# MLA attention on one core: products of P with V of two query tiles in one place of TensorE's order, and transposed P copied back into its own tile

## The chip, the cores and the metric

The kernel runs on one core of a Trainium2 chip. The metric is device time in microseconds for one execution, the median over several runs. The profile is of one execution of the same program.

## The reference, cut to what matters

One residual block of an encoder, 512 tokens, width 1024: attention in two head groups side by side (8 MLA heads of 96/64, 4 differential heads), output projection, a gated convolutional feed-forward part, and a gate from per-layer embeddings. The change touches the MLA heads alone:

```python
q = rms_norm(q, q_g); k = rms_norm(k, k_g)          # 8 heads, 96 wide
q, k = rope on the last 32 columns of each
scale = MLA_QK ** -0.5
allowed = (k_idx[None, :] // CHUNK) <= (q_idx[:, None] // CHUNK)   # CHUNK = 64
logits = einsum('bhqd,bhkd->bhqk', qb, k_t) * scale
logits = where(allowed, logits, NEG_INF)
probs = softmax(logits, axis=-1)
o = einsum('bhqk,bhkd->bhqd', probs, v_t)            # v is 64 wide
```

All in float32, with `SEQ = 512`, `D_MODEL = 1024`, `MLA_HEADS = 8`, `MLA_QK = 96`, `MLA_V = 64`.

## The kernel before, in words

**Tiles and steps.** The 512 queries are four tiles of 128 (t = 0 to 3). By the mask, tile t needs the first (t + 1) * 128 keys. Heads go in pairs (hp = 0 to 3), the two heads of a pair are c = 0, 1. The loop at L840 goes over hp and t; step i = 4hp + t does, in the program's order:

1. `mla_norm` (DVE, L614): P of tile t is multiplied by the reciprocal of its row sums.
2. `mla_logits` of the next tile (TensorE through `mm3`, L157 to L159: three products a block, because each operand is a high and a low part; bank `ml`), and DVE's row maxima (L587 or L590, then L588 or L591).
3. `mla_exp` (ACT, L605): exponentials into the P tile `pm`, with row sums. At t = 2, heads of the next pair are transposed and split between them (`mla_q`, `mla_k`, L559 and L566, banks of the tag `tp`; splits by ACT L185, L188 and DVE L186, L189), at t = 3 two more. In the last pair the first transposes and logits of the differential heads stand there (`d0T`, `d1T` L715, `dl`).
4. `extra` work of that step (splits of later weights L305, squares and scalings of the differential heads' z, L407 and L414), then `pump(n)`: products of the projection z of the differential heads (`zd`, six products of 512 columns each pump) that fill TensorE's time; n is 2 in pairs 0 to 2 and 1 in the last.
5. `mla_T`: P of tile t is transposed on TensorE (L547, bank `pTm`), each head's P in its own bank, or both heads in one bank for t < 2 (`one`). It is copied to a tile `pt` (L550 by ACT, L552 by DVE).
6. `mla_pv` of the tile of the step before (L633): 64-wide V is the stationary operand, transposed P the moving one; head c fills partitions 64c to 64c + 63 of the bank `mo`. A block of 128 keys is four instructions in the trace (two heads, two passes each). After t = 3 ACT copies the bank to `ym` (L636).

**Buffers.** `pm` tiles come from four buffers in a ring (`pm_tile`), `pt` tiles from two (`pt_tile`). A tile with t < 2 takes one of each, a tile with t > 1 two of each. After the loop the differential heads use both rings for their own P.

**What sets the order.** TensorE runs in the order of the program for the whole kernel. DVE, ACT and POOL do so from L217 to L888, which holds this whole stage; a planner places what the program issues after that, and it can put such instructions in idle places of ACT's order inside the stage (casts of the output projection's weights, L150, come from there). DMAs of weights are issued by SP; none is issued by the functions that the diff touches.

Of the kernel before, what the change touches and what calls it, by code (L numbers as in the profile page):

```python
# [22 lines left out]
NT = 4  # L23
# [4 lines left out]
H = 8  # L28
# [66 lines left out]
def hybrid_block(ctx: ExitStack, tc: tile.TileContext, a: dict, out: bass.AP):  # L95
    nc = tc.nc
    V, S, G, TE = nc.vector, nc.scalar, nc.gpsimd, nc.tensor
# [13 lines left out]
    def bank(tag, name):  # L111
        return pp_.tile([P, 512], F32, tag=tag, bufs={"acc": 2, "lg": 3, "tp": 2, "ob": 1}[tag], name=name)

    def tt(name, dtype=F32):
        return att.tile([P, T], dtype, tag="tt", bufs=16, name=name)
# [4 lines left out]
    def pm_tile(name):  # L120
        return att.tile([P, T], F32, tag="pm", bufs=PM, name=name)

    def pt_tile(name):
        return att.tile([P, T], F32, tag="pt", bufs=2, name=name)
# [29 lines left out]
    def mm3(ps, blocks, first=True, last=True, again=False):  # L154
        n = len(blocks)
        for i, (xh, xl, wh, wl) in enumerate(blocks):
            TE.matmul(ps, xh, wh, start=first and i == 0, stop=False, skip_group_check=again)  # L157
            TE.matmul(ps, xh, wl, start=False, stop=False, skip_group_check=again)  # L158
            TE.matmul(ps, xl, wh, start=False, stop=last and i == n - 1, skip_group_check=again)  # L159
# [31 lines left out]
    tsl = [slice(t * P, (t + 1) * P) for t in range(NT)]  # L191
# [208 lines left out]
    def z_flush():  # L400
        while zouts:
            zouts.pop(0)()
# [37 lines left out]
    def pump(n=1):  # L440
        for _ in range(n):
            while fill:
                try:
                    next(fill[0])
                    break
                except StopIteration:
                    fill.pop(0)
# [37 lines left out]
    qn, kv = [], []  # L485
# [54 lines left out]
    pump(FILL_QK)  # L540


    def probs_T(pm, n, name, on_act):

        ps = bank("tp", f"pT{name}")
        for j in range(0, n, P):
            TE.transpose(ps[:, j:j + P], pm[:, j:j + P], ident)  # L547
        pt = pt_tile("pt")
        if on_act:
            S.copy(pt[:, :n], ps[:, :n])  # L550
        else:
            V.tensor_copy(pt[:, :n], ps[:, :n])  # L552
        return pt

    def mla_q(h):
        qh_, ql_, kh_, kl_ = QT[h % 2]
        ps = bank("tp", f"qT{h}")
        for t in range(NT):
            TE.transpose(ps[:QK, tsl[t]], qn[t][:, h, :], ident)  # L559
        split(qh_[:QK], ql_[:QK], ps[:QK], qcol[:QK])  # L560

    def mla_k(h):
        qh_, ql_, kh_, kl_ = QT[h % 2]
        ps = bank("tp", f"kT{h}")
        for t in range(NT):
            TE.transpose(ps[:QK, tsl[t]], kv[t][:, h, :QK], ident)  # L566
        split(kh_[:QK], kl_[:QK], ps[:QK])

    mla, ymn = {}, []

    def mla_logits(hp, t):

        n, one = (t + 1) * P, t < 2
        r = rq[:, 0, t, 2 * hp:2 * hp + 2]
        sums = sm.tile([P, 3, 2], F32, tag="sums", bufs=4, name="sums")
        nm = sums[:, 0]
        ps, pm = [], []
        for c in range(2):
            qh_, ql_, kh_, kl_ = QT[c]
            if c and one:  # L580
                ps.append(full[:, n:2 * n])
            else:
                full = bank("lg", f"ml{hp}{t}{c}")
                ps.append(full[:, :n])
            mm3(ps[c], [(qh_[:100, tsl[t]], ql_[:100, tsl[t]], kh_[:100, :n], kl_[:100, :n])])
            if not one:
                V.reduce_max(nm[:, c:c + 1], ps[c], axis=AX.X, negate=True)  # L587
                V.tensor_tensor(nm[:, c:c + 1], nm[:, c:c + 1], r[:, c:c + 1], op=ALU.mult)  # L588
        if one:
            V.reduce_max(nm, full[:, :2 * n].rearrange("p (c k) -> p c k", c=2), axis=AX.X, negate=True)  # L590
            V.tensor_tensor(nm, nm, r, op=ALU.mult)  # L591
        mla["lg", hp, t] = ps, nm, r
        for c in range(2):
            if c and one:
                pm.append(pmf[:, n:2 * n])
            else:
                pmf = pm_tile("pm")
                pm.append(pmf[:, :n])
        mla["pm", hp, t] = pm, pmf, sums, one

    def mla_exp(hp, t, c):

        ps, nm, r = mla["lg", hp, t]
        pm, pmf, sums, one = mla["pm", hp, t]
        S.activation(pm[c], ps[c], AF.Exp, bias=nm[:, c:c + 1], scale=r[:, c:c + 1], accum_out=sums[:, 1, c:c + 1])  # L605

    def mla_norm(hp, t):

        pm, pmf, sums, one = mla["pm", hp, t]
        ssum, rcp = sums[:, 1], sums[:, 2]  # L610
        for c in range(2):
            if c == 0:
                V.reciprocal(rcp, ssum)
            V.tensor_scalar(pm[c], pm[c], rcp[:, c:c + 1], None, op0=ALU.mult)  # L614

    def mla_T(hp, t):

        n = (t + 1) * P
        pm, pmf, sums, one = mla.pop(("pm", hp, t))
        if one:  # L620
            pt = probs_T(pmf, 2 * n, f"m{hp}{t}", t)
            mla["pt", hp, t] = [pt[:, :n], pt[:, n:2 * n]]
        else:
            mla["pt", hp, t] = [probs_T(pm[c], n, f"m{hp}{t}{c}", c) for c in range(2)]

    def mla_pv(hp, t):

        if t == 0:
            mla["po"] = bank("ob", f"mo{hp}")
        po, pt = mla["po"], mla.pop(("pt", hp, t))  # L630
        for j in range(t + 1):
            for c in range(2):
                TE.matmul(po[64 * c:64 * c + 64, tsl[t]], kv[j][:, 2 * hp + c, 96:], pt[c][:, tsl[j]], start=j == 0, stop=j == t)  # L633
        if t == NT - 1 and hp < H // 2 - 1:
            yn = tt(f"ym{hp}")
            S.copy(yn, po)  # L636
            ymn.append(yn)
# [82 lines left out]
    def diff_logits(h, t):  # L720
        n = (t + 1) * P
        if t == 0:
            df["s0", h] = sm.tile([P, NT], F32, tag="s0", name="s0")
        s0 = df["s0", h][:, t:t + 1]
        (qh_, ql_), (kh_, kl_) = df["qk", h, 0], df["qk", h, 1]
        pms, s1 = [], sm.tile([P, 1], F32, tag="s1", bufs=4, name="s1")
        for m in range(2):
            r = slice(64 * m, 64 * m + 64)
            ps = bank("lg", f"dl{h}{t}{m}")
            mm3(ps[:, :n], [(qh_[r, tsl[t]], ql_[r, tsl[t]], kh_[r, :n], kl_[r, :n])])  # L730
            pm = pm_tile("pmd")
            nm = sm.tile([P, 1], F32, tag="nm", bufs=4, name="nmd")
            V.tensor_tensor_reduce(out=pm[:, :n], in0=ps[:, :n], in1=strips[0][:, h, T - n:], scale=1.0, scalar=3e38, op0=ALU.add, op1=ALU.min, accum_out=nm)  # L733
            S.activation(pm[:, :n], pm[:, :n], AF.Exp, bias=nm, scale=-1.0, accum_out=s0 if m == 0 else s1)  # L734
            pms.append(pm)
        df["pm", h, t] = pms, n, s0, s1
# [53 lines left out]
    HP = H // 2  # L790
# [44 lines left out]
    z13 = z1_hi(3)  # L835
    pump()
    mla_logits(0, 0)
    for c in range(2):
        mla_exp(0, 0, c)
    for hp in range(HP):  # L840
        for t in range(NT):
            i = NT * hp + t
            last = hp == HP - 1
            n = FILL_MLA[hp][t]
            if t:
                mla_norm(hp, t)
            if t < NT - 1:
                mla_logits(hp, t + 1)
            if t == 2:
                for c, (d, m) in enumerate(((diff_T, (0, 0)), (diff_T, (0, 1))) if last else ((mla_q, (2 * hp + 2,)), (mla_k, (2 * hp + 2,)))):  # L850
                    d(*m)
                    mla_exp(hp, t + 1, c)
            elif t < 2:
                for c in range(2):
                    mla_exp(hp, t + 1, c)
            else:
                pump()
                n -= 1
                if last:
                    diff_logits(0, 0)  # L860
                else:
                    mla_q(2 * hp + 3)
                    mla_k(2 * hp + 3)
            if t == 0:
                mla_norm(hp, t)
            for e in extra.get(i, ()):
                e()
            pump(n)
            for e in late.get(i, ()):
                e()  # L870
            mla_T(hp, t)
            z_flush()
            if i:
                mla_pv(*divmod(i - 1, NT))
            if t == 3 and not last:
                mla_logits(hp + 1, 0)
                for c in range(2):
                    mla_exp(hp + 1, 0, c)
# [49 lines left out]
    for b in order[:6]:  # L928
        n = len(early)
# [359 lines left out]
    ts = [token_sums(k) for k in range(K2)]  # L1289
# [279 lines left out]
```

## Time and profile before

| what | value |
|---|---|
| median of 3 runs | 644.8 us (644.76 to 645.9) |
| the profiled execution | 644.82 us |
| its span in the trace | 643.0 us |
| TensorE matmul busy | 632.4 us, 98% |
| DVE, ACT, POOL busy | 486.9, 360.2, 69.2 us |
| products with V in the trace (L633) | 160 instructions, first 78.6, last 156.2 us |
| transposes of P of the MLA heads (L547, pTm) | 80 instructions, 73.8 to 153.0 us |
| granted TensorE clock | full in all slices |

A line of the timeline gives the start, the busy time, the engine, the line of the kernel, the operation, tile written and tiles read, the shape, how many instructions are merged, and in brackets the idle time of the engine before it with what ended it. PE is TensorE's products, PEld its weight loads, DVE is VectorE, ACT ScalarE. The ends of products are modelled, so starts are the better measure there.

### The profile page before, as it was taken

The page shows a single profiled execution, that of the slowest core. Times are in us where ns is not written, and L with a number is a line of the kernel's source. Part 1 is how long each engine was busy: PE and PEld are TensorE (multiplying, and loading weights), DVE is VectorE, ACT ScalarE, POOL GpSimd, SP SyncE. Part 2 cuts the span into 40 slices and gives each one's busy share as a digit, 9 for nine tenths or more (in the row PEclk, how much of TensorE's full clock was granted, in tenths as well). Part 3 has the DMA queues.
Part 4 walks back from the last instruction along what each step waited for, and adds up shares of the span by engine and source line. Part 5 has one row for each costly group of instructions (what it writes and reads, how often), then busy time and mean ns, then how long its engine had stood idle before and what let it go on. Part 6 is the DMA issues. An engine that isn't in the chain of part 4 may idle for free.

```text
span 643.0 us, 10203 instructions
## 1 busy us (share of the span) xinstructions
PE 632.4 (98%) x3900; PEld 556.2 (87%) x3900; DVE 486.9 (76%) x870; ACT 360.2 (56%) x629; POOL 69.2 (11%) x94
## 2 busy tenths in 40 slices
PE   8999999999999999999999999999999999999997
PEld 8988888876777887889999999999999999988886
DVE  6889667887898678988876767676767777759844
ACT  7896567666667355557555545545454545637111
POOL 1514103030000130001000000000100000000000
PEclk9999999999999999999999999999999999999999
DMA  8241612330221437546865656464646554532021
GB/s 304 100 165 37 182 62 66 99 130 2 66 85 49 164 132 228 148 95 157 208 197 117 184 124 199 117 180 116 180 115 182 118 177 115 181 130 66 27 88 50
DMA packets 29912, 82.63 MB, mean 129 GB/s; under 512 B 3100, under 2 KB 4124, under 8 KB 29736
## 3 DMA queue, kind: packets, MB, share of 16 engines
q1 hardware_dynamic: 23816, 69.17, 32.3%
q0 software_dynamic: 5616, 12.33, 11.3%
q8 instruction: 31, 0.51, 0.3%
q10 hardware_dynamic: 432, 0.49, 0.2%
q14 instruction: 17, 0.14, 0.1%
HBM read 77.77 MB, written 5.52 MB: 130 GB/s over the span
## 4 chain that ended last, share of the span: by engine, by line
PE 86%; DVE 7%; ACT 3%; issue 2%; DMA 1%; ACTq 0%; DVEq 0%; SPq 0%
PE dn L157 6%; PE dn L158 6%; PE dn L159 6%; PE gx L159 4%; PE gx L158 4%; PE gx L157 4%; PE zd L157 3%; PE zd L159 3%; PE zd L158 3%; PE g L157 3%; PE g L158 3%; PE g L159 3%; PE pg L159 2%; PE pg L158 2%; PE pg L157 2%; PE o L157 2%
## 5 line engine op out<-in xcount | busy, mean ns | idle before, releaser
L954 DVE TENSOR_TENSOR wSl<-rS,wSh 128x1024 fp32r<-128x1024 f32 x21 | 25.7, 1224 | 43.4 <-ACT wSh L950 43.2
L157 PE MATMUL dn<-ah,hi_dn 128*128 128x512 f32 x144 | 56.2, 391 | 0.0
L158 PE MATMUL dn<-al,hi_dn 128*128 128x512 f32 x144 | 56.2, 391 | 0.0
L159 PE MATMUL dn<-ah,lo_dn 128*128 128x512 f32 x144 | 56.0, 389 | 0.0
L1071 POOL DMA_DIRECT2D rS<-in_w_gu x19 | 22.7, 1194 | 250.2 <-DVE cv L1239 129.9
L950 ACT CAST wSh<-rS 128x1024 fp32r<-128x1024 f32 x21 | 22.0, 1047 | 35.7 <-PE gy L158 35.4
L157 PE MATMUL zd<-hi_d,xh 128*128 128x512 f32 x96 | 39.1, 407 | 0.0
L158 PE MATMUL zd<-lo_d,xh 128*128 128x512 f32 x96 | 37.6, 392 | 0.0
L682 DVE TENSOR_TENSOR x<-x,dn 128x512 f32<-128x512 f32 x44 | 29.9, 679 | 6.1 <-PE dn L159 6.1
L954 DVE TENSOR_TENSOR wTl<-rA,wTh 128x1024 fp32r<-128x1024 f32 x19 | 23.3, 1225 | 13.7 <-ACT wTh L950 13.2
L159 PEld LDWEIGHTS dn<-ah,lo_dn 128*128 128x128 f32 x144 | 27.0, 188 | 5.8
L157 PEld LDWEIGHTS dn<-ah,hi_dn 128*128 128x128 f32 x144 | 27.1, 188 | 5.1
L158 PEld LDWEIGHTS dn<-al,hi_dn 128*128 128x128 f32 x144 | 27.1, 188 | 5.0
L954 DVE TENSOR_TENSOR wAl<-rA,wAh 128x1024 fp32r<-128x1024 f32 x21 | 25.6, 1217 | 2.7 <-ACT wAh L950 2.7
L950 ACT CAST wAh<-rA 128x1024 fp32r<-128x1024 f32 x21 | 22.1, 1050 | 9.7 <-DMA rA<-in_w_gu 9.5
L1242 ACT ACTIVATE cv<-cv 128x512 f32<-128x512 f32 x22 | 13.9, 630 | 23.9 <-DVE cv L1239 23.8
L157 PE MATMUL g<-b2h,wAh 128*128 128x256 f32 (+1 forms) x88 | 26.4, 300 | 0.5 <-ACT g L1195 0.5
L157 PE MATMUL o<-yh,hi_o 128*128 128x512 f32 x64 | 26.8, 419 | 0.0
L734 ACT ACTIVATE pmd<-pmd,nmd 128x128 f32<-128x128 f32 (+3 forms) x32 | 17.9, 560 | 15.1 <-DVE nmd L733 15.0
L159 PE MATMUL g<-b2h,wAl 128*128 128x256 f32 (+1 forms) x88 | 26.2, 297 | 0.0
L158 PE MATMUL g<-b2l,wAh 128*128 128x256 f32 (+1 forms) x88 | 26.2, 297 | 0.0
L1462 ACT ACTIVATE sg<-sg 128x512 f32<-128x512 f32 (+1 forms) x9 | 5.3, 584 | 36.8 <-DVE sg L1461 36.8
(475 smaller groups left out, 2219.1 us busy)
## 6 DMA issues: line engine op xcount, KB each, us to landing
rA<-in_w_gu SPq DMA_DIRECT2D x22, 512.0 KB, 3.7
rS<-in_w_gu SPq DMA_DIRECT2D x22, 512.0 KB, 3.7
rS<-in_w_gu POOLq DMA_DIRECT2D x19, 512.0 KB, 6.1
raw_dn<-in_w_down SPq DMA_DIRECT2D x18, 512.0 KB, 5.9
raw_d<-in_w_d SPq DMA_DIRECT2D x12, 512.0 KB, 3.4
r<-in_w_gu SPq DMA_DIRECT2D x19, 256.0 KB, 5.9
raw_o<-in_w_out SPq DMA_DIRECT2D x8, 512.0 KB, 3.6
rS_pg<-in_w_pg SPq DMA_DIRECT2D x6, 512.0 KB, 4.1
```

Of the source, the lines that this page charges most:

```text
L157: TE.matmul(ps, xh, wh, start=first and i == 0, stop=False, skip_group_check=again)
L158: TE.matmul(ps, xh, wl, start=False, stop=False, skip_group_check=again)
L159: TE.matmul(ps, xl, wh, start=False, stop=last and i == n - 1, skip_group_check=again)
L682: V.tensor_tensor(xb(b), xb(b), ps, op=ALU.add)
L734: S.activation(pm[:, :n], pm[:, :n], AF.Exp, bias=nm, scale=-1.0, accum_out=s0 if m == 0 else s1)
L950: S.copy(h_, src)
L954: V.tensor_tensor(l_, src, _f32(h_), op=ALU.subtract)
L1071: nc.gpsimd.dma_start(sums[f].rearrange("p (i c) -> p i c", i=2), a["w_gu"][f][:, :2048].rearrange("p (i c) -> p i c", i=2)[:, :, :512], a ...
L1242: S.activation(cv, cv, AF.Silu)
L1462: S.activation(sg, sg, AF.Sigmoid)
```

## The change

`mla_pv` takes several tiles, and a table says at which step which tiles' products with V are issued: tiles 0 and 1 at step 4hp + 2, tiles 2 and 3 at step 4hp + 4, in the last pair tile 2 at step 15 and tile 3 behind the loop, as before. So tile 0's and tile 2's products move one step back. Transposed P has to live longer for this. For t < 2, P is now made in a `pt` tile, and its transpose is copied back into it; for t > 1 it is copied back into its two `pm` tiles, except in the last pair, where two `pt` tiles take it as before.

```diff
-    def probs_T(pm, n, name, on_act):
+    def probs_T(pm, n, name, on_act, pt=None):
...
-        pt = pt_tile("pt")
+        pt = pt_tile("pt") if pt is None else pt
...
-                pmf = pm_tile("pm")
+                pmf = pt_tile("pm") if one else pm_tile("pm")
...
-            pt = probs_T(pmf, 2 * n, f"m{hp}{t}", t)
+            pt = probs_T(pmf, 2 * n, f"m{hp}{t}", t, pmf)
...
-            mla["pt", hp, t] = [probs_T(pm[c], n, f"m{hp}{t}{c}", c) for c in range(2)]
+            mla["pt", hp, t] = [probs_T(pm[c], n, f"m{hp}{t}{c}", c, pm[c] if hp < H // 2 - 1 else None) for c in range(2)]
...
-    def mla_pv(hp, t):
+    def mla_pv(hp, *ts):
-        if t == 0:
+        if ts[0] == 0:
             mla["po"] = bank("ob", f"mo{hp}")
-        po, pt = mla["po"], mla.pop(("pt", hp, t))
-        for j in range(t + 1):
-            for c in range(2):
-                TE.matmul(po[64 * c:64 * c + 64, tsl[t]], kv[j][:, 2 * hp + c, 96:], pt[c][:, tsl[j]], start=j == 0, stop=j == t)
-        if t == NT - 1 and hp < H // 2 - 1:
+        po = mla["po"]
+        for t in ts:
+            pt = mla.pop(("pt", hp, t))
+            for j in range(t + 1):
+                for c in range(2):
+                    TE.matmul(po[64 * c:64 * c + 64, tsl[t]], kv[j][:, 2 * hp + c, 96:], pt[c][:, tsl[j]], start=j == 0, stop=j == t)
+        if ts[-1] == NT - 1 and hp < H // 2 - 1:
...
+    pvs = {NT * hp + 2: (hp, 0, 1) for hp in range(HP)} | {NT * hp + 4: (hp, 2, 3) for hp in range(HP - 1)} | {NT * HP - 1: (HP - 1, 2)}
...
-            if i:
-                mla_pv(*divmod(i - 1, NT))
+            if i in pvs:
+                mla_pv(*pvs[i])
```

## The prediction

> **What bounds the kernel now.** I read the page's summary first, then the waits of TensorE, then a table of busy time by stretches, and only then the timeline of the stage that is changed.
>
> ```profile
> span 643.0 us, 10203 instructions
> ...
> PE 632.4 (98%) x3900; PEld 556.2 (87%) x3900; DVE 486.9 (76%) x870; ACT 360.2 (56%) x629; POOL 69.2 (11%) x94
> ...
> PE 86%; DVE 7%; ACT 3%; issue 2%; DMA 1%; ACTq 0%; DVEq 0%; SPq 0%
> ```
>
> TensorE is busy 98% of the span, and 86% of the chain that ended last is TensorE. A time taken out of TensorE's order is therefore a time taken out of the run, unless TensorE then meets a wait. Where it waits today, the view of waits for TensorE says (us in total, times, longest):
>
> ```profile
> PE mo L633 <- DVE pt L552: 0.7, 1, 0.7
> ...
> PE pTm L547 <- DVE st L189: 0.4, 1, 0.4
> PE pTm L547 <- DVE pm L614: 0.3, 1, 0.3
> ```
>
> These three are the only waits at the lines of the change (transposes of P, L547, and products with V, L633). The table of busy time by stretches puts them (columns: stretch, its length, then busy us of each engine):
>
> ```profile
> 118.00:139.00 21.00, 21.00 (x142) 16.98 (x140) 17.12 (x40) 13.97 (x28) 5.80 (x1) 1.00 0.45 148
> 139.00:157.00 18.00, 16.52 (x132) 12.73 (x132) 13.51 (x38) 12.62 (x32) 0.00 (x0) 1.00 0.02 5
> 157.00:220.00 63.00, 61.39 (x372) 48.68 (x371) 53.51 (x150) 39.09 (x97) 4.03 (x4) 1.00 0.24 78
> 220.00:643.00 423.00, 417.20 (x2608) 376.96 (x2606) 311.95 (x432) 210.75 (x316) 27.89 (x23) 1.00 0.50 140
> ```
>
> Up to 139 us, through head pairs 0 to 2, TensorE has no idle time. In 139 to 157, head pair 3, it is idle 1.48 of 18 us: there ACT and DVE set the end. After 157 it is busy again 97 to 99%. So a gain before 139 should count in full, one after it should not, and what is gained by 157 should last to the end.
>
> **What a separate group of products with V costs.** The timeline of TensorE around three places (start, us, what, how many):
>
> ```profile
> 78.06 0.60 PE L547 MATMUL pTm<-ident,pm 128*128 128x128 f32 x4
> 78.59 0.44 PE L633 MATMUL mo<-pt,kvb 128*64 128x128 f32 x4
> 78.96 0.50 PE L157 MATMUL ml<-st 100*128 100x512 f32 x1
> 79.30 0.39 PE L158 MATMUL ml<-st 100*128 100x512 f32 x1
> ...
> 84.10 0.82 PE L547 MATMUL pTm<-ident,pm 128*128 128x128 f32 x6
> 84.84 0.66 PE L633 MATMUL mo<-pt,kvb 128*64 128x128 f32 x8
> 85.43 0.50 PE L157 MATMUL zd<-hi_d,xh 128*128 128x512 f32 x1
> 85.77 0.40 PE L158 MATMUL zd<-lo_d,xh 128*128 128x512 f32 x1
> ...
> 87.37 0.60 PE L566 MATMUL kT<-ident,kvb 128*96 128x128 f32 x4
> 87.72 0.48 PE L157 MATMUL zd<-hi_d,xh 128*128 128x512 f32 x1
> 88.04 0.40 PE L158 MATMUL zd<-lo_d,xh 128*128 128x512 f32 x1
> ```
>
> The third place has four transposes and then a 512-wide product, with no product with V between: 88.04 - 87.37 = 0.67 us from the first transpose to the second wide product. The first place has the same with four product instructions (tile t=0) between: 79.30 - 78.06 = 1.24, so that group costs 0.57. The second has six transposes, 85.77 - 84.10 = 1.67; two transposes more at 0.11 (x4 lasts 0.60, x6 lasts 0.82) make its base 0.89, so its eight instructions (t=1) cost 0.78. From 0.57 to 0.78 are four instructions more: 0.21 to 0.22 for each key block of 128. What is left when the work is taken off is 0.57 - 0.22 = 0.35 and 0.78 - 0.44 = 0.34: a fixed price of about 0.35 us for going from full-width work to 64-wide work and back. The weight loads show where it sits:
>
> ```profile
> 84.84 0.42 PEld L633 LDWEIGHTS mo<-pt,kvb 128*64 128x64 f32 x8 [0.17 <-issue]
> 85.43 0.19 PEld L157 LDWEIGHTS zd<-hi_d,xh 128*128 128x128 f32 x1 [0.17 <-issue]
> ...
> 87.70 0.19 PEld L157 LDWEIGHTS zd<-hi_d,xh 128*128 128x128 f32 x1
> ```
>
> Before the first 64-wide load and before the first full-width load after it nothing is loaded for 0.17 us, with no releaser; from transposes straight to wide products (87.70) there is no such hole. 2 x 0.17 = 0.34 is the fixed price again. Within a group of eight no hole is shown, although it changes column halves and key blocks, so a second query tile appended should cost its 0.22 per block alone.
>
> [...]
>
> **The change part by part.** Steps are i = 4hp + t, 0 to 15.
>
> Products. Before there are 16 groups, one a tile. After there are nine: pairs at i = 2, 4, 6, 8, 10, 12, 14, tile (3,2) alone at 15, tile (3,3) alone behind the loop. Seven groups go (those at i = 1, 3, ..., 13), each to the step behind it; no instruction is added. Gross: 7 x 0.35 = 2.4 us. The moved products (t=0: 0.22, t=2: 0.65 us) pass logits, fill products and transposes on TensorE and nothing on another queue: no DMA belongs to them, SP and POOL issue the same, and the copy of the finished bank to ym stays at its step.
>
> Copies of transposed P. Same engine, same shape, other destination: 0 (a 512-wide one lasts 0.69 on DVE, below, either way). What hides it is that both tiles lie in SBUF; I know no reason for a price of either sign. Their waits change: in head pairs 0 to 2 the copies no longer wait until the products of an earlier tile have freed one of two pt tiles. That gives DVE and ACT time early in a step, which matters below. In head pair 3, tiles 2 and 3 still copy into pt; the copy of (3,2) by DVE now waits for (3,0)'s products, which stand just behind the transposes: 0 to 0.2 us, covered by another split that keeps DVE until then.
>
> New holds. P of tiles 2 and 3 keeps its pm tiles until the pair's products at i = 4hp + 4. The next writer is the exponential of (hp+1, 2), whose logits come later in TensorE's order than those products: 0. For the bank mo the hold is shorter. Behind the waiting exponential on ACT nothing waits longer than it does for the logits.
>
> **Where the 0.35 does not arrive.** At odd i = 3, 7, 11 the products of tile 2 stood between the transposes and the next head pair's logits. Without them logits begin 1.0 us earlier (0.65 work + 0.35), and the next transposes are reached 1.0 earlier, but they need the normalization that DVE makes from those logits. DVE's and TensorE's rows at i = 4, 8 and 12, in that order:
>
> ```profile
> 91.18 0.69 DVE L552 COPY pt<-pTm 128x512 f32<-128x512 f32 x1 [0.96 <-PE mo L633]
> ```
> ```profile
> 113.66 0.69 DVE L552 COPY pt<-pTm 128x512 f32<-128x512 f32 x1 [0.42 <-PE mo L633]
> ...
> 116.42 0.48 DVE L614 TENSOR_SCALAR pm<-pm,sums 128x128 f32<-128x128 f32 x2
> ```
> ```profile
> 117.80 0.38 PE L547 MATMUL pTm<-ident,pm 128*128 128x128 f32 x2
> ```
> ```profile
> 136.14 0.69 DVE L552 COPY pt<-pTm 128x512 f32<-128x512 f32 x1 [0.35 <-PE mo L633]
> 136.96 0.42 DVE L590 TENSOR_REDUCE sums<-ml 128x2 f32<-128x256 f32 x1
> ...
> 140.82 0.43 DVE L552 COPY pt<-pTm 128x256 f32<-128x256 f32 x1 [0.23 <-PE mo L633]
> ...
> 141.89 0.55 DVE L587 TENSOR_REDUCE sums<-ml 128x1 f32<-128x384 f32 x1
> ...
> 147.67 0.74 DVE L189 SCALAR_TENSOR_TENSOR st<-d0T,dcol,st 128x512 fp32r<-128x512 f32 x1
> ```
> ```profile
> 139.33 0.43 PE L547 MATMUL pTm<-ident,pm 128*128 128x128 f32 x2 [0.26 <-DVE pm L614]
> ...
> 140.72 0.44 PE L157 MATMUL ml<-st 100*128 100x384 f32 x1
> ...
> 141.17 0.34 PE L159 MATMUL ml<-st 100*128 100x384 f32 x1
> ...
> 148.47 1.19 PE L547 MATMUL pTm<-ident,pm 128*128 128x128 f32 x6 [0.38 <-DVE st L189]
> ...
> 155.45 1.09 PE L633 MATMUL mo<-pt,kvb 128*64 128x128 f32 x16 [0.74 <-DVE pt L552]
> ```
>
> i = 8: the copy can start its idle 0.42 earlier, and DVE's chain with it, so normalization ends at 116.90 - 0.42 = 116.5. TensorE arrives at 117.80 - 1.0 = 116.8. Still covered by 0.3, and the full 0.35 counts. At i = 4 DVE idles 0.96 before the copy, and its chain can follow almost the whole 1.0.
>
> i = 12: today TensorE already waits 0.26. DVE gains only its idle 0.35 and the 0.13 between the copy's end (136.83) and the reduction (136.96), so the transposes start about 0.45 earlier instead of 1.0; then 0.65 of tile 2's products follow, and the next logits (140.72) come 0.2 later than now. DVE's reduction of them (141.89) starts 0.38 after the first logits are done (141.51), held by DVE's own queue, so it still comes about 0.1 earlier. At i = 13 TensorE saves 0.57, but the transposes of i = 14 (148.47) wait for DVE's split of d0T already and follow DVE: 0.1 earlier. Tile (3,0)'s 0.22 is added there, which leaves 0.1 later; the wait at 155.45 hangs on a chain that begins with logits of that step and moves alike.
>
> Sum: five groups x 0.35 = 1.75, less 0.1 for the last two, 1.6 to 1.7 us gained by 157 us. The profiled execution took 644.82 (span 643.0 and 1.82 around it): 644.82 - 1.65 = 643.2. The median of the runs, 644.8, is the same to 0.02. From both sides: if nothing of the last head pair is lost, 2.4 gained, 642.4; if its waits of 0.26 and 0.38 also shrink, to 641.8. If only the groups at i = 1, 5, 9 (no logits chain near) count, 3 x 0.35 = 1.05, 643.8.
>
> **The rivals.** (a) All seven count, 642.4 or somewhat lower. For it: ACT's order in the last head pair holds a cast that is not of this stage,
>
> ```profile
> 143.47 1.05 ACT L150 CAST hi_o<-raw_o 128x1024 fp32r<-128x1024 f32 x1
> 144.42 0.67 ACT L605 ACTIVATE pm<-ml,sums,rq 128x384 f32<-128x384 f32 x1
> ```
>
> between the two exponentials of tile (3,2). It is an instruction of the next stage, put there by the planner; if the planner puts it elsewhere, the chain to 148.47 shortens by up to 1.05. Against it: nothing in the change asks for that.
>
> (b) No change that can be measured, 643.6 to 645. Either a wait at i = 4 or 8 that I called covered opens, up to 0.35 each, with one cast of (a) more in the last chain (1.65 - 0.7 = 0.95 left); or the change doesn't do what it says, and every tile's products cost the 0.35 even when they stand together. Against the latter: the hole stands at the ends of a group of eight and not within it. [...] The rows at 84.84 and 85.43 don't bear it out at this switch; 3 in 100.
>
> (c) Slower. The planner orders ACT from the second stage on, and three such casts of 1.05 stand inside this stage. If the new order puts two more of them before exponentials of head pair 3, where TensorE waits for ACT and DVE, 2 x 1.05 = 2.1 is lost against 1.65: 645.3. It decides from the second cast on; one alone leaves a gain of 0.6 (644.2). For it: one stands there now. Against: it takes two moves of the planner to the same short stretch of 18 us, where ACT is idle 5.4 us (12.62 busy) and could take a cast at no cost.
>
> **How the numbers follow.** My forecast has 52 in 100 (642.8 to 643.6), (a) 17, (b) 23, (c) 8. A difference of 0.2%, 1.3 us, is about what a measurement of this kernel can tell from none, so faster means under 643.5 and slower over 646.1. Of the forecast 46 of 52 lie under 643.5, and all of (a): 0.63. Two casts too many give 645.3 and a third 646.4, so I put 5 of (c)'s 8 to slower and 3 to no change: 0.05, and 0.32 is left for no change. The range reaches from (a) with shrunken waits, 642.0, to the larger part of (b), 644.5; the forecast's own range is 642.8 to 643.6.
>
> **What would show it.** Right: weight loads at L633 with holes of 0.17 nine times and not 16; transposes at i = 1, 3, 5, ... followed at once by logits; the stage's end (the last group of sixteen products, now 155.45) at about 153.8; the same distance as now from there to the end. The last head pair: a wait of about 0.8 instead of 0.26 before the transposes of (3,0). Wrong: new idle time of TensorE before transposes at i = 4 or 8 (DVE's chain is not covered), holes inside a pair, a different ACT order in the last head pair, or an end of the stage that is earlier while the end of the run is not.

## The result and the profile after

The changed kernel takes 642.18 us (median of 6 runs, 641.95 to 643.07), the kernel before beside it 644.78 (6 runs). The ratio is 0.9963, 95% interval 0.9953 to 0.9973. In a later set of runs it is 0.9971 (0.9962 to 0.9981). So it is faster by 0.3 to 0.4%, 1.8 to 2.6 us by the two sets' medians. 643.2 was forecast. The measured time lies in the range that was given, 642.0 to 644.5, but below the forecast's own, 642.8 to 643.6, and nearer to rival (a) with 642.4. The sign and the price of a group are right; what the last head pair adds is not.

The page of the changed kernel:

```profile
span 640.6 us, 10207 instructions
...
PE 630.7 (98%) x3900; PEld 557.3 (87%) x3900; DVE 486.4 (76%) x870; ACT 360.0 (56%) x629; POOL 68.5 (11%) x94
```

The instruction counts of all five engines are those of before; TensorE's matmul time is 1.7 us less. Its waits at the lines of the change, in the view of waits of the changed kernel:

```profile
PE mo L635 <- DVE pt L552: 0.7, 1, 0.7
PE pTm L547 <- DVE pm L614: 0.6, 1, 0.6
...
PE pTm L547 <- DVE st L186: 0.5, 1, 0.5
```

All three are in head pair 3, as before. The timeline of TensorE at steps 1 and 2 (where the prediction read the price of a group), and the weight loads there:

```profile
78.50 0.60 PE L547 MATMUL pTm<-ident,pm 128*128 128x128 f32 x4
78.85 0.48 PE L157 MATMUL ml<-st 100*128 100x512 f32 x1
79.17 0.40 PE L158 MATMUL ml<-st 100*128 100x512 f32 x1
...
83.96 0.82 PE L547 MATMUL pTm<-ident,pm 128*128 128x128 f32 x6
84.70 0.88 PE L635 MATMUL mo<-pm,kvb 128*64 128x128 f32 x12
85.51 0.50 PE L157 MATMUL zd<-hi_d,xh 128*128 128x512 f32 x1
```
```profile
78.27 0.58 PEld L547 LDWEIGHTS pTm<-ident,pm 128*128 128x128 f32 x4
78.82 0.19 PEld L157 LDWEIGHTS ml<-st 100*128 100x128 f32 x1
...
84.70 0.64 PEld L635 LDWEIGHTS mo<-pm,kvb 128*64 128x64 f32 x12 [0.17 <-issue]
85.51 0.19 PEld L157 LDWEIGHTS zd<-hi_d,xh 128*128 128x128 f32 x1 [0.17 <-issue]
```

Step 1 now takes 79.17 - 78.50 = 0.67 us from the transposes to the second wide product, the base without a group, to the hundredth; it was 1.24. The twelve products of tiles 0 and 1 at step 2 have one hole before and one behind, none between the tiles: from 84.70 to 85.51 is 0.81, where eight took 0.59 and the four more add 0.22. In the whole stage weight loads for products with V start a group nine times and not 16: eight times behind a hole of 0.12 to 0.17 us, and once in the wait before the last group.

To compare kernels I use three starts on TensorE, since this stage does not begin at the same time in all profiles (from 74.02 us in `lastapart` to 75.91 in `apart`): the first transposes of P (step 0), the transposes of tile (2,3) (step 11), and the first product of the output projection behind the stage. In the kernel before, then in the changed one:

```profile
74.05 0.38 PE L547 MATMUL pTm<-ident,pm 128*128 128x128 f32 x2
...
134.16 1.14 PE L547 MATMUL pTm<-ident,pm 128*128 128x128 f32 x8
...
156.89 0.47 PE L157 MATMUL o<-yh,hi_o 128*128 128x512 f32 x1
```
```profile
74.50 0.38 PE L547 MATMUL pTm<-ident,pm 128*128 128x128 f32 x2
...
132.92 1.15 PE L547 MATMUL pTm<-ident,pm 128*128 128x128 f32 x8
...
155.17 0.47 PE L157 MATMUL o<-yh,hi_o 128*128 128x512 f32 x1
```

Part A (step 0 to 11) went from 60.11 to 58.42 us, part B (step 11 to the end of the stage) from 22.72 to 22.25, together 82.84 to 80.68. So 2.16 us are gained in the stage, 1.69 in A and 0.47 in B. (Parts and differences are taken from unrounded starts, so their last digit can differ by one from what the rows give.) The same numbers for all kernels, from their timelines, with the medians and the ratio to the kernel before in the same set of runs:

| kernel | groups | A | B | stage | median us | ratio (95%) |
|---|---|---|---|---|---|---|
| before | 16 | 60.11 | 22.72 | 82.84 | 644.8 | |
| changed | 9 | 58.42 | 22.25 | 80.68 | 642.18 | 0.9963 (0.9953 to 0.9973) |
| changed_again | 9 | 58.41 | 22.26 | 80.68 | 642.64 | 0.9971 (0.9962 to 0.9981) |
| apart | 16 | 60.13 | 21.60 | 81.73 | 643.09 | 0.9979 (0.9969 to 0.9988) |
| copyback | 16 | 60.15 | 22.71 | 82.87 | 644.70 | 1.0004 (0.9996 to 1.0013) |
| lastapart | 10 | 58.41 | 22.61 | 81.02 | 642.89 | 0.9977 (0.9967 to 0.9988) |
| castlate | 16 | 60.09 | 22.60 | 82.69 | 644.35 | 0.9996 (0.9987 to 1.0005) |
| castearly | 9 | 58.43 | 22.92 | 81.35 | 643.21 | 0.9976 (0.9966 to 0.9987) |
| ahead | 9 | 58.41 | 21.28 | 79.70 | 641.21 | 0.9947 (0.9935 to 0.9959) |
| quad | 6 | 56.70 | 22.03 | 78.74 | 640.37 | 0.9935 (0.9923 to 0.9947) |
| quadlate | 6 | 56.70 | 21.32 | 78.02 | 639.32 | 0.9925 (0.9911 to 0.9938) |
| quadsplit | 6 | 56.72 | 22.42 | 79.13 | 640.31 | 0.9936 (0.9923 to 0.9949) |

The changed kernel twice gives the same part A and B to 0.01 us, and all kernels with nine or ten groups have the same A to 0.02 us. So here a profile tells 0.1 us, while the gains by the medians of two sets of runs, 2.6 and 1.8, are 0.8 apart.

### The profile page after: what moved, and what is told of

It reads as the page before. It is cut to its first block, busy times and chain, and to the rows that moved or that the text cites. A ratio compares the mean times of both kernels' runs of the same rounds, so it can differ in the third digit from the quotient of the medians.

```text
span 640.6 us, 10207 instructions
## 1 busy us (share of the span) xinstructions
PE 630.7 (98%) x3900; PEld 557.3 (87%) x3900; DVE 486.4 (76%) x870; ACT 360.0 (56%) x629; POOL 68.5 (11%) x94
## 4 chain that ended last, share of the span: by engine, by line
PE 86%; DVE 7%; ACT 3%; issue 2%; DMA 1%; ACTq 0%; DVEq 0%; SPq 0%
PE dn L157 6%; PE dn L158 6%; PE dn L159 6%; PE gx L159 4%; PE gx L158 4%; PE gx L157 4%; PE zd L157 3%; PE zd L159 3%; PE zd L158 3%; PE g L157 3%; PE g L158 3%; PE g L159 3%; PE pg L159 2%; PE pg L158 2%; PE pg L157 2%
```

## The experiments

**Is it the number of groups, or the later steps and the freed copies?** Two kernels. In `apart` the pair's first tile stands ahead of the step's transposes:

```diff
+            two = pvs.get(i, ())
+            if len(two) == 3:
+                mla_pv(*two[:2])
+                two = two[0], two[2]
             mla_T(hp, t)
             z_flush()
-            if i in pvs:
-                mla_pv(*pvs[i])
+            if two:
+                mla_pv(*two)
```

> The changed kernel, but in each step that holds a pair the first tile's products stand ahead of that step's transposes and the second tile's behind them. Same steps, buffers and copies as the changed kernel, but 16 groups of products again. If the gain is the fixed price of a group (two holes of 0.17 us), it goes: 7 x 0.35 = 2.4 us more than the changed kernel, 644.2 to 645.0 us, with 16 pairs of holes in TensorE's weight loads. If the gain comes from the later steps, or from copies that wait for less, it stays: 642.0 to 642.6.

In `copyback` only buffers and copies are those of the change:

```diff
-    pvs = {NT * hp + 2: (hp, 0, 1) ...
+    pvs = {i: divmod(i - 1, NT) for i in range(1, NT * HP)}
```

> The copies into the P tiles of the changed kernel alone, products of each tile one step after their transposes as in the kernel before. If only the number of groups counts: 644.8, at most 0.4 less, because DVE copies earlier where it idled 0.35 and 0.23 us (at the steps around head pair 3). If copies that wait for less carry the gain: 642.2 to 643.

Part A of `apart` is 60.13, the 60.11 of before: with 16 groups again, at the same later steps and with the same buffers, all of A's gain is gone. `copyback` has 60.15 and 22.71: copies back into P's own tile cost nothing and bring nothing. So the gain of A is the number of groups: 1.69 us for five of them, 0.34 each. (The profile of `apart` shows a granted clock of 0.95 and the others 1.0, but its fill products follow each other in the same 0.228 us, five steps from 84.05 to 85.19 us as from 82.59 to 83.73 in the changed kernel, so its parts are compared as they stand.)

But `apart` is not slow as a whole. Its median is 643.09, between the two expectations, because part B is 21.60, shorter than in the changed kernel. There the first tile's products stand where TensorE waited in head pair 3: the wait before the transposes of (3,0) and those before the transposes of (3,2) are gone from its trace, and of the stage's waits only this one is left:

```profile
156.19 1.11 PE L635 MATMUL mo<-pt,kvb 128*64 128x128 f32 x16 [0.71 <-DVE pt L552]
```

I had not expected that; it led to `ahead`, below.

**The last head pair.** `lastapart` gives tiles (3,0) and (3,1) two steps again:

```diff
-    pvs = {NT * hp + 2: (hp, 0, 1) for hp in range(HP)} | ...
+    pvs = {NT * hp + 2: (hp, 0, 1) for hp in range(HP - 1)} | ... | {NT * HP - 3: (HP - 1, 0), NT * HP - 2: (HP - 1, 1), NT * HP - 1: (HP - 1, 2)}
```

> The changed kernel, but in head pair 3 tiles 0 and 1 have their products in two steps as before (10 groups instead of nine). By the prediction's step for the last pair TensorE only follows DVE there, and nothing is lost: 642.2, with the end of the stage in the trace within 0.1 us of the changed kernel's. If each group counts its 0.35 there too: 642.5, with the end of the stage 0.35 us later.

Part B is 22.61, 0.36 longer than in the changed kernel: the group at step 13 counts in full, and for it the prediction's step does not hold. (The medians can't tell: 642.89 here, 642.18 and 642.64 for the changed kernel.) What the prediction used was TensorE waiting for DVE's split at the transposes of (3,2). The engines' orders in this stage show what moved between the kernel before and the changed one: DVE and POOL have the same order in both; ACT has one instruction elsewhere, the third cast of output weights. In the changed kernel it stands behind both exponentials of tile (3,2):

```profile
141.10 0.67 ACT L605 ACTIVATE pm<-ml,sums,rq 128x384 f32<-128x384 f32 x1 [0.91 <-DVE sums L588]
...
141.82 0.67 ACT L605 ACTIVATE pm<-ml,sums,rq 128x384 f32<-128x384 f32 x1
...
142.48 1.03 ACT L150 CAST hi_o<-raw_o 128x1024 fp32r<-128x1024 f32 x1
```

The other group that goes from B, at step 11, brings nothing, as forecast. The transposes of tile (3,1), in the kernel before and in the changed one, start

```profile
143.27 0.60 PE L547 MATMUL pTm<-ident,pm 128*128 128x128 f32 x4
```
```profile
142.01 0.60 PE L547 MATMUL pTm<-ident,pm 128*128 128x128 f32 x4
```

9.11 and 9.09 us behind those of tile (2,3), with the same work on TensorE between; the wait before the transposes of (3,0) grew instead.

`castearly` is the changed kernel with that cast written out in the old place (the two casts ahead of it are written out too, and keep their places):

```diff
...
                 for c in range(2):
                     mla_exp(hp, t + 1, c)
+                    if i == 13 and c == 0:
+                        w_hi(3)
```

> The changed kernel, but the three casts of output weights are written into ACT's order by hand, the third one between the two exponentials of tile (3,2), where the kernel before has it and the changed one has not. If the cast's new place is why the last pair gained more than forecast, the end of the stage comes 0.3 to 0.5 us later than in the changed kernel: 642.5 to 642.7. If DVE and ACT follow TensorE there whatever the cast does: 642.2, same end of the stage.

Part B becomes 22.92, 0.67 longer, more than the 0.3 to 0.5 expected, and the whole stage 81.35. TensorE in the changed kernel, then ACT and TensorE in `castearly`:

```profile
146.12 0.53 PE L547 MATMUL pTm<-ident,pm 128*128 128x128 f32 x3
147.19 0.55 PE L547 MATMUL pTm<-ident,pm 128*128 128x128 f32 x3 [0.55 <-DVE st L186]
```
```profile
141.88 1.05 ACT L810 CAST hi_o<-raw_o 128x1024 fp32r<-128x1024 f32 x1 [0.35 <-PE zd L159]
142.84 0.67 ACT L605 ACTIVATE pm<-ml,sums,rq 128x384 f32<-128x384 f32 x1
```
```profile
146.88 1.19 PE L547 MATMUL pTm<-ident,pm 128*128 128x128 f32 x6 [0.71 <-DVE st L189]
```

With the cast between, the first head's transposes wait 0.71 for the chain exponential, normalization, split; without it they don't wait, and only the second head's do, 0.55. Nothing else differs in DVE's, ACT's or POOL's order in this stage, so with nine groups the cast's place is worth 0.67 us. (The cast also starts 0.35 late here, behind a fill product; in `copyback` it does so too, and B is not longer there.)

Is that place worth as much without the change? `castlate` is the kernel before with that cast put behind the second exponential:

```diff
-                with tc.issue_after(df["comb"].ins):
+                with tc.issue_after(df["comb"].ins), tc.issue_after(mla["exp", HP - 1, 2, 1].ins) if dq == 2 else ExitStack():
                     wo_first[0, dq + 1] = wo_w(0, dq + 1)
```

> The kernel before, with one thing moved: on ACT the cast of output weights (1.05 us) that stands between the two exponentials of tile (3,2) comes behind the second one. Nothing else differs in any engine's order. If that place cost time in the last head pair, the waits of 0.38 us and of the next transposes shrink: the end of the stage comes 0.4 to 0.7 us earlier, 644.1 to 644.4. If it cost nothing, 644.8 and the same waits.

The stage is 0.14 shorter, 0.12 of it in B, not 0.4 to 0.7. The first head's wait of 0.38 went, but the second head's transposes, which waited 0.10, now wait 0.58 for the split of d1T:

```profile
149.50 0.55 PE L547 MATMUL pTm<-ident,pm 128*128 128x128 f32 x3 [0.58 <-DVE st L186]
```

So in part B the two can't be put to separate accounts: fewer groups alone lose 0.20 there (`castearly`), the cast's place alone gains 0.12, and both together gain 0.47.

**Products ahead of the transposes.** `ahead` is the changed kernel with `mla_pv` called before `mla_T` in head pair 3:

> The changed kernel, but in head pair 3 the products with V stand ahead of the transposes of their step, so that they fill TensorE's waits for DVE (0.59 and 0.55 us in the changed kernel). Still nine groups. If those waits were idle time that only the order makes, 0.5 to 1.0 us less than the changed kernel: 641.2 to 641.7. If the transposes, now later, only push the copies and the last products (they wait 0.73 for a copy) back by the same: 642.2.

It measures 641.21, and part B is 21.28, 0.97 shorter than in the changed kernel. The waits before the transposes are gone; the one before the last products grew from 0.73 to 0.89:

```profile
152.28 1.09 PE L635 MATMUL mo<-pt,kvb 128*64 128x128 f32 x16 [0.89 <-DVE pt L552]
```

The idle time was of the order's making. (The cast stands between the exponentials in this kernel, so its gain is not the cast's; in `apart` it stands behind them.)

**Longer groups.** `quad` puts all four tiles of a pair into step 4hp + 4, ahead of the fill products, with a separate ring for tile 0's P, and takes the order of `ahead` in the last pair:

```diff
+    def pt0_tile(name):
+        return att.tile([P, 2 * P], F32, tag="pt0", bufs=2, name=name)
...
-                pmf = pt_tile("pm") if one else pm_tile("pm")
+                pmf = pt0_tile("pm") if t == 0 else pt_tile("pm") if one else pm_tile("pm")
...
-    pvs = ...
+    pvs = {NT * hp + 4: (hp, 0, 1, 2, 3) for hp in range(HP - 1)} | {NT * HP - 2: (HP - 1, 0, 1), NT * HP - 1: (HP - 1, 2)}
...
+            if hp and t == 0:
+                mla_pv(*pvs[i])
             pump(n)
...
+            if i in pvs and t:
+                mla_pv(*pvs[i])
             mla_T(hp, t)
             z_flush()
-            if i in pvs:
-                mla_pv(*pvs[i])
```

> All four tiles of a head pair in one group at step 4hp + 4, ahead of that step's fill products; in head pair 3 tiles 0 and 1 at step 14 and tile 2 at step 15, ahead of the transposes. Tile 0 has a ring of its own (two tiles 256 wide). Six groups, three fewer than the changed kernel: 3 x 0.35 = 1.05 us less, and the last pair's waits as in the kernel before this one, 0.5 to 1.0: 640.2 to 641.2. If the price per group does not go on falling with longer groups, or DVE falls behind: 641.2 to 642.2.

640.37, ratio 0.9935. Part A is 56.70, 3.41 less than before. Of that, 0.66 is work that has only moved to B (tiles (2,0) and (2,1), six instructions of each head at 0.11), and eight groups less make 2.75, 0.34 each. The price of a group did not change with its length: a group of 40 instructions still has it once.

```profile
92.14 2.40 PE L638 MATMUL mo<-pm,kvb 128*64 128x128 f32 x40
```

Two kernels on what is left in its part B. `quadlate` moves the cast as in `castlate`:

> The kernel with four tiles in a group, and on ACT the third cast of output weights behind the second exponential of tile (3,2) instead of between the two; no other engine's order differs. In the changed kernel that cast's place was worth 0.67 us of the stage, because TensorE waited there. Here TensorE waits 0.2 us before the transposes of (3,2), (3,3) and of d1, so the theory allows 0.2 us at most: 640.2 to 640.4. If the cast costs its own time wherever it stands: 639.7.

639.32, ratio 0.9925, the fastest here. The stage is 0.72 shorter than in `quad`, where I had allowed 0.2: this expectation was wrong. The waits that the trace of `quad` shows before the transposes of d1 and of (3,2) are 0.12 and 0.09, but the starts say more. In `quad`, then in `quadlate`:

```profile
143.34 0.60 PE L720 MATMUL d0T<-ident,zd 128*128 128x128 f32 x4
144.06 0.66 PE L720 MATMUL d1T<-ident,zd 128*128 128x128 f32 x4
```
```profile
141.94 0.60 PE L720 MATMUL d0T<-ident,zd 128*128 128x128 f32 x4
142.38 0.60 PE L720 MATMUL d1T<-ident,zd 128*128 128x128 f32 x4
```

From the one start to the next are 0.72 and 0.44 us, so the wait costs 0.28 and the trace calls it 0.12: idle time is counted from the modelled end of the last product, and where nothing waits the next starts before it (in `quadlate` at 142.38, 0.16 ahead of the end at 142.54). At the transposes of (3,2) it is 0.30 for a shown 0.09, and the last wait (0.88 to 0.80) makes most of the rest.

`quadsplit` makes the two splits of attention outputs one step earlier (`late` at 13 and 14 instead of 14 and 15):

> The kernel with four tiles in a group, and the splits of the first two attention outputs (0.6 us on ACT, 0.69 on DVE each) one step earlier, so that at step 15 none of them stands ahead of DVE's copy of (3,3), for which TensorE waits 0.88 us. If the split ahead of the copy makes that wait, it shrinks by 0.5 to 0.7 us: 639.7 to 639.9. If the copy waits for something else, or the splits now delay the normalization of the step before: 640.4 or more.

The wait of 0.88 before the last products is gone from its trace, so the split ahead of DVE's copy did make it. But two others opened upstream, and the stage is 0.39 longer than in `quad`; the median, 640.31, does not change:

```profile
143.19 0.66 PE L720 MATMUL d1T<-ident,zd 128*128 128x128 f32 x4 [0.64 <-ACT pm L553]
...
146.54 1.19 PE L550 MATMUL pTm<-ident,pm 128*128 128x128 f32 x6 [0.49 <-DVE st L192]
```

The split's cast on ACT now stands ahead of the copy that frees a bank for d1's transposes. The wait moved, and grew.

`changed_again` is the changed kernel beside `castearly`, `ahead` and `quad`:

> The changed kernel once more, beside the three others on one chip: 642.2 us by its first runs, 2.4 under the kernel before if seven groups of 0.35 us all count, 1.65 under it if the last pair's two do not.

642.64, which is 1.84 under the kernel before it, and the same stage as its first profile, 80.68. By medians this set is nearer to 1.65 and the first, with 2.6, to 2.4; the stage says 2.16.

## Why the prediction was right, and where not

- **Price of a group, 0.35 us, none inside a longer group: right.** 0.34 by five groups (changed), 0.34 by eight (`quad`), back with 16 groups (`apart`). Seven times 0.34 is 2.37, where the rows made 2.4. In rival (b), the 3 in 100 were for a switch without a hole to save; the loads above show 0.17 before the group at 84.70 and 0.17 behind it.
- **Copies and buffers at 0: right**, by `copyback` (0.03 us).
- **The cover at i = 4 and 8: right.** No wait of TensorE before step 12, and A's five groups count 1.69 of the forecast 1.75.
- **The last head pair: the term of the sum that was mis-sized.** Forecast 0.1 lost, measured 0.47 gained. With the cast where I took it to stay, the order behind the forecast, it is 0.20 lost (`castearly`), and the stage's gain is 1.48 where 1.65 was forecast. So the working of that step held for the order that it assumed, and the planner's order was not that one. A different order of ACT there was named as a sign of being wrong, and it came. Rival (a) named this cast and its place; I gave it 17 in 100, since nothing in the change asks for it. Its number, 642.4, lies between the two medians measured, but its count did not hold: of the seven groups the one at step 11 brought nothing, and the stage gained 2.16 and not 2.4. That the last group starts at 153.74, where about 153.8 was forecast, is chance: this execution reached the stage 0.45 us later than the profile before. That this order came from the change through the planner is shown by the order itself, the same in both profiles of the changed kernel; why the planner took it is not.
- **The step's mechanism, "follows DVE", was too rigid.** With the cast out of the chain, TensorE's order counts there again (0.36 for one group, `lastapart`), and the wait goes on to the second head's split (0.55).
- **The wait before (3,0):** forecast about 0.8, shown 0.59. By the starts in the changed kernel's timeline it is near 0.8:

```profile
132.68 0.40 PE L159 MATMUL zd<-hi_d,xh3l 128*128 128x512 f32 x1
132.92 1.15 PE L547 MATMUL pTm<-ident,pm 128*128 128x128 f32 x8
...
136.45 0.39 PE L159 MATMUL zd<-hi_d,xh5l 128*128 128x512 f32 x1
137.43 0.44 PE L547 MATMUL pTm<-ident,pm 128*128 128x128 f32 x2 [0.59 <-DVE pm L614]
```

From the last fill product to the transposes are 0.98 us at step 12 and 0.24 at step 11, which has no wait, so TensorE lost 0.74.

- **What was gained by 157 lasts to the end: right to what a profile can tell.** From the end of the stage to the end of the span the kernel before takes 486.1, the changed one 485.4 (span less the start of the first output product). The other profiles scatter as far, and the ranges overlap (485.3 to 486.3 with 16 groups, 485.4 to 485.9 with nine or ten, 485.0 to 485.3 with six), so I count none of the 0.7. What makes this scatter stays open.

## What to carry to other kernels

In these traces, a group of 64-wide products (128*64 in the rows) among 128-wide work cost a hole of about 0.17 us on the way in and another on the way out, 0.34 us together, with four instructions in it as with 40. So count such groups, not the products, and put the narrow products together where their operands can live that long. Where TensorE already waited for another engine, a group's place mattered too (0.97 us in `ahead`, with the nine groups of the changed kernel): work that is ready belongs ahead of the instruction that waits. And a planner's order belongs to the prediction: the place of one cast, between two exponentials or behind them, was worth 0.67 us, almost two groups, in one order and 0.14 in another.

## What the runs showed of the hardware that was not expected

The idle time that these traces show before a product is shorter than the wait in the three places compared: 0.12 shown for 0.28 lost, 0.09 for 0.30, 0.59 for 0.74. So waits of TensorE are better read from starts here.

The hole stands at the 64-wide products and not wherever a product is two instructions in the trace: the differential heads' products with V (`do`), two instructions as well but 128 wide, and from the same kind of tile, follow transposes without one in the trace of the kernel before.

```profile
196.12 0.38 PE L547 MATMUL pTd<-ident,pmd 128*128 128x128 f32 x2
196.34 0.39 PE L752 MATMUL do<-zd,pt 128*128 128x128 f32 x2
196.65 0.32 PE L157 MATMUL dl<-st 64*128 64x128 f32 x1
```

The two transpose instructions take 0.22, 0.11 each as within a run of them, and the products start right behind them.

The products `dl`, which use 64 rows where the others above use 128 or 100, have such a hole behind transposes too. Their weight loads come 0.17 us late there, all seven times in the trace of the kernel before:

```profile
192.36 0.19 PEld L157 LDWEIGHTS dl<-st 64*128 64x128 f32 x2 [0.17 <-issue]
```

Loads with 100 rows (`ml` at 78.82 in the changed kernel, above) show none behind transposes.
